# A fused two-layer decoder kernel: the norm's split by 256-column parts, high parts first, and the output by parts

## The chip, the cores and the metric

The kernel runs as one program on one core of one Trainium2 chip. The metric is the device time of one execution in microseconds (us); the figure for the kernel before is the median of three runs. The core's engines are PE (TensorE, matrix multiplication), DVE (VectorE), ACT (ScalarE), POOL (GpSimd) and SP (SyncE, which here only issues DMAs).

## The reference

Two layers over 256 rows of 1024 columns, in float32. `moba`, `nsa` and `gla` stand for three kinds of attention; their insides don't matter here.

```python
def rms_norm(x, gain):
    xf = x.astype(jnp.float32)
    y = xf * lax.rsqrt(jnp.mean(xf * xf, axis=-1, keepdims=True) + NORM_EPS)
    return (y * gain.astype(jnp.float32)).astype(x.dtype)
```

Each layer computes `h = rms_norm(x)`, one wide projection of h for all branches, the three branches, `z = sum_i sigmoid(gate_i(h)) * (branch_i @ P_i)` and `x = x + z @ W_out`; then `x = x + ConvFFN(rms_norm(x))`, where the FFN projects up to 2 x 2816 columns, convolves and gates them, and projects down by `w_down`. The result is x after the second layer.

## The kernel before

x lives in SBUF as `xs`, 128 partitions x 2 row tiles t x 1024 columns. Each float32 product runs on PE as three matmuls on rounded operands: high by high, high by low and low by high. For weights, SP loads a block `raw` of 1024 elements per partition, ACT casts it to `whi`, and DVE or POOL or both subtract to get `wlo`; a rule in the planner (`low`, L303) cuts the columns between the two. For activations, `hh` is the high and `hl` the low part of the turned, gain-scaled x.

A phase is a list of chunks (a 512- or 256-column piece of a weight matrix); `run_phase` (L407) walks over blocks of k-tiles, three matmuls per k-tile and piece, and after each k step calls `tick()`, which advances the generators in the lists `urgent` and `normal`. Everything that isn't a main matmul is such a generator: the work of a chunk's end (`done_...`), the splits, the attention. Its `yield from avail(...)` or `ready(...)` waits until a planner's clock (class `Plan`, L51, with a cost per instruction) says that the data will be there; so the planner's costs decide after which matmul the generator's instructions are put. The order of each engine's instructions is thus fixed when the program is built, and hardware semaphores do the waiting. All instructions are recorded through one helper, so every one has line L163 in the profile; tiles tell them apart.

The order of chunks in the up projection is `split_order(3, 4)`: the first four k-tiles of three chunks, then their last four. So k-tiles 0 to 3 are needed first, and all of the first half's work comes from columns 0 to 511 of x. The input projection of layer 1 uses `split_order(2, 4)`; the output projection `split_order(2, 4)`, the down projection chunk after chunk.

The change touches the seam between two projections. `done_out` (L1426) is the end of a chunk of the output projection (w_out) or the down projection (w_down): for half c (512 columns) it adds the two PSUM banks `pd` (one for each t) to `xs`, then runs `nxt(c)`, which is `after_mixer` (L1437) or `after_ffn` (L1442). Both run `norm_half` (L641): for each of two parts j of 256 columns, i.e. two k-tiles, it takes a bank `pst` (semaphore `sem_ps`, three banks), lets PE turn the part (`x_T`, L624, four transposes), and splits k-tile by k-tile: `norm_hi` (ACT, hh), `norm_lo` (DVE, hl), and again. Then `norm_sq` (L658) squares the half's columns on ACT, and after the second half `norm_rs` (L665) makes the root (POOL) and turns it (PE). After the last layer, `after_ffn` issues the output DMAs instead, one for each t.

Four places are meant below. A: 229 to 250 us, from layer 0's output projection to its up projection. B: 426 to 470, from its down projection to layer 1's input projection. C: 643 to 664, as A in layer 1. D: the end.

Of the kernel before, what the change touches and what calls it, by code (L numbers as in the profile page):

```python
# [13 lines left out]
OP = mybir.AluOpType  # L14
# [166 lines left out]
def trunk_kernel(ctx, tc, x, rel_bias, attn_norm, w_in, moba_q_norm, moba_k_norm,  # L181
# [19 lines left out]
    sem_pd, sem_po, sem_ps, sem_t = Sem(4), Sem(1), Sem(3), Sem(NT)  # L201

    def take(s, n=1):
        while True:
            t = s.at(n)
            if t is not None and t <= plan.t["PE"]:
                break
            plan.step = max(plan.step, t or 0.0)
            yield
        s.take(n)  # L210

    def give(s, n=1):
        s.free += [plan.step] * n
# [4 lines left out]
    def pst():  # L218
        return ps.tile([128, 512], F32, name="pst", tag="pst")

    def tt():
        return tp.tile([128, 512], F32, name="tt", tag="tt", bufs=NT)

    plan = Plan()
    V, A, G, PE, SP = (Eng(plan, e, g) for e, g in (("V", nc.vector), ("A", nc.scalar), ("G", nc.gpsimd),
                                                    ("PE", nc.tensor), ("S", nc.sync)))

    def avail(*aps):
        while max(plan.get(a) for a in aps) > plan.t["PE"]:
            plan.step = max([plan.step] + [plan.get(a) for a in aps])  # L230
            yield
# [7 lines left out]
    def bc(ap, shape):  # L239
        return ap.to_broadcast(shape)  # L240
# [98 lines left out]
    urgent, normal = [], []  # L339
    flags = set()  # L340
# [53 lines left out]
    def wait(*fl):  # L394
        for f in fl:
            while f not in flags:
                yield
# [88 lines left out]
    xs = cst.tile([128, 2, D], F32, name="xs")  # L486
# [127 lines left out]
    def norm_state(key):  # L614
        st = {}
        st["h"] = hp.tile([128, 8, S], F32R, name="hh", tag="hh")
        st["l"] = hp.tile([128, 8, S], F32R, name="hl", tag="hl")
        st["ss"] = at.tile([128, 2, 2], F32, name="ss", tag="ss", bufs=2)
        st["rs"] = at.tile([128, 2], F32, name="rs", tag="rs", bufs=2)
        st["rsh"] = at.tile([128, 2], F32, name="rsh", tag="rsh", bufs=2)  # L620
        st["rsB"] = at.tile([128, 1, S], F32, name="rsB", tag="rsB", bufs=2)
        st["key"] = key
        return st

    def x_T(c):

        p = pst()
        for k in range(2):
            for t in range(2):
                PE.transpose(p[:, k * 256 + t * 128:k * 256 + t * 128 + 128],  # L630
                             xs[:, t, c * 256 + k * 128:c * 256 + k * 128 + 128], ident)
        return p

    def norm_hi(st, c, k, p, g):
        A.activation(st["h"][:, 2 * c + k], p[:, k * 256:k * 256 + 256], AF.Copy, scale=g[:, 2 * c + k:2 * c + k + 1])

    def norm_lo(st, c, k, p, g):
        V.scalar_tensor_tensor(st["l"][:, 2 * c + k], p[:, k * 256:k * 256 + 256], g[:, 2 * c + k:2 * c + k + 1],
                               st["h"][:, 2 * c + k].bitcast(F32), op0=OP.mult, op1=OP.subtract)

    def norm_half(st, c, l, goff):  # L641

        yield from wait(("par", l))
        g = par[l][0][:, goff:goff + 8]
        for j in (2 * c, 2 * c + 1):
            yield from take(sem_ps)
            p = x_T(j)
            yield
            for k in range(2):
                norm_hi(st, j, k, p, g)  # L650
                norm_lo(st, j, k, p, g)
            give(sem_ps)
            flags.add((st["key"], j))
        yield from norm_sq(st, c)
        if c:
            yield from norm_rs(st)

    def norm_sq(st, c):  # L658
        yield from take(sem_t)
        q = tt()  # L660
        for t in range(2):
            A.activation(q, xs[:, t, c * 512:c * 512 + 512], AF.Square, accum_out=st["ss"][:, t, c:c + 1])
        give(sem_t)

    def norm_rs(st):  # L665
        ms = at.tile([128, 2], F32, name="ms", tag="ms", bufs=2)
        V.tensor_tensor(ms, st["ss"][:, :, 0], st["ss"][:, :, 1], op=OP.add)
        V.tensor_scalar(ms, ms, 1.0 / D, EPS, op0=OP.mult, op1=OP.add)
        G.tensor_tensor(st["rs"], ms, mhalf[:, :2], op=OP.pow)
        yield  # L670
        yield from avail(st["rs"])
        V.tensor_scalar(st["rsh"], st["rs"], 0.5, None, op0=OP.mult)
        flags.add((st["key"], "rs"))
        yield from take(sem_ps)
        p = pst()
        for t in range(2):
            PE.transpose(p[:, t * 128:t * 128 + 128], bc(st["rs"][:, t:t + 1], [128, 128]), ident)
        yield
        A.copy(st["rsB"][:, 0], p[:, :256])
        give(sem_ps)  # L680
        flags.add((st["key"], "rsB"))
# [10 lines left out]
    def make_layer(l):  # L692
        key = lambda *a: (l,) + a
        st = {}
# [728 lines left out]
                give(sem_t, 2)  # L1423
            return f

        def done_out(c, nxt):  # L1426
            def f(p):
                for t in range(2):
                    xv = xs[:, t, c * 512:c * 512 + 512]
                    V.tensor_tensor(xv, p[t], xv, op=OP.add)  # L1430
                give(sem_pd, 2)
                yield
                yield from avail(*(xs[:, t, c * 512:c * 512 + 512] for t in range(2)))
                yield from nxt(c)
            return f

        def after_mixer(c):  # L1437
            if "n2" not in st:
                st["n2"] = norm_state(key("n2"))
            yield from norm_half(st["n2"], c, l, 8)  # L1440

        def after_ffn(c):  # L1442
            if l + 1 < L:
                nx = layers[l + 1]
                if "n1" not in nx["st"]:
                    nx["st"]["n1"] = norm_state((l + 1, "n1"))
                yield from norm_half(nx["st"]["n1"], c, l + 1, 0)
            else:
                o2 = out.rearrange("b (t p) d -> p (b t) d", p=128)
                for t in range(2):  # L1450
                    SP.dma_start(o2[:, t, c * 512:c * 512 + 512], xs[:, t, c * 512:c * 512 + 512])
                yield


# [71 lines left out]
        for c in range(2):  # L1526
            for br, (w, nk, kx, fl_) in enumerate(((w_branch_moba, 2, 0, "moba"), (w_branch_nsa, 2, 2, "nsa"),
# [3 lines left out]
                                   lambda k, fl_=fl_: key(fl_)))  # L1531
        ph_out = [Chunk("A", 512, 8, wload(w_out[l], [(c * 512, 512)]), lambda: (st["zh"], st["zl"], 0),
                        done_out(c, after_mixer), lambda k: key(("z", k // 2))) for c in range(2)]
        ph_up = []
        for j in range(11):
# [119 lines left out]
    for l, ly in enumerate(layers):  # L1655
        st = ly["st"]
# [12 lines left out]
    k = 0  # L1669
# [51 lines left out]
```

## Time and profile before

| | |
|---|---|
| median of 3 runs | 843.26 us (842.91 to 844.48) |
| profiled execution | 844.73 us |
| its span in the profile | 842.9 us |
| mean granted TensorE clock | 0.996 |
| PE busy | 831.8 us (99%) |
| DVE busy | 571.0 us (68%) |
| ACT busy | 430.1 us (51%) |
| POOL busy | 418.0 us (50%) |

Times inside the profile count from the span's start. An idle time in brackets behind a row is that of the engine just before the instruction, with the instruction that ended it. Matmuls overlap in the record: one of 512 columns is shown with 0.39 us, but the next starts 0.23 later. The granted clock is the share of TensorE's full 2.4 GHz; 0.50 is 1.2 GHz.

### The profile page before, as it was taken

The numbers are of one execution on the slowest core, as the hardware profiler recorded it, in microseconds if no ns is written. First come the engines' busy times: TensorE is split into PE (matmuls) and PEld (weight loads), VectorE is DVE, ScalarE is ACT, GpSimd is POOL, SyncE is SP. The second block draws the span as 40 slices with busy tenths as digits, with TensorE's granted clock in tenths as the row PEclk, the third lists the DMA queues.
The fourth block names the chain that finished last, engine by engine and source line by source line (L and its number), as shares of the span: only waits on it lengthen the run. The fifth ranks groups of instructions, "written<-read, shape, count | busy, mean of one in ns | idle before, by whom it ended". The sixth has DMA issues, their size and how long they took to land.

```text
span 842.9 us, 13919 instructions
## 1 busy us (share of the span) xinstructions
PE 831.8 (99%) x5173; PEld 741.0 (88%) x5173; DVE 571.0 (68%) x880; ACT 430.1 (51%) x667; POOL 418.0 (50%) x338
## 2 busy tenths in 40 slices
PE   8999999999999999999999999999999999999998
PEld 7789888888899999988897898888887999999886
DVE  4676887458657888774457478766585688777642
ACT  5565546554456544544456444655544664545431
POOL 2435653456535655565425265435564265665652
PEclk9999999999999999999999999999999999999999
DMA  6893534545545656655568435434556556665560
GB/s 212 234 317 108 152 114 131 150 165 185 180 147 180 197 176 175 201 179 199 156 178 245 128 100 150 130 121 150 181 174 196 153 165 188 196 184 190 191 210 26
DMA packets 109976, 143.57 MB, mean 170 GB/s; under 512 B 13677, under 2 KB 71380, under 8 KB 109780
## 3 DMA queue, kind: packets, MB, share of 16 engines
q1 hardware_dynamic: 109892, 142.68, 54.7%
q8 instruction: 41, 0.67, 0.3%
q14 instruction: 27, 0.22, 0.1%
q10 hardware_dynamic: 16, 0.00, 0.0%
HBM read 141.60 MB, written 2.63 MB: 171 GB/s over the span
## 4 chain that ended last, share of the span: by engine, by line
PE 91%; DVE 3%; issue 2%; POOL 2%; ACT 1%; DMA 0%; SPq 0%; POOLq 0%; DVEq 0%; ACTq 0%
PE pd L163 80%; PE pst L163 9%; PE po L163 2%; POOL wlo L163 2%; DVE wlo L163 1%; ACT whi L163 1%; DVE tt L163 1%; DVE xs L163 0%; POOL tt L163 0%; DVE hl L163 0%; ACT hh L163 0%; DVE boot L163 0%; DVE m L163 0%; DMA tt<-in_moba_k_norm_dram 0%; DVE kn L163 0%
## 5 line engine op out<-in xcount | busy, mean ns | idle before, releaser
L163 ACT CAST whi<-raw 128x1024 fp32r<-128x1024 f32 (+3 forms) x268 | 271.4, 1017 | 285.1 <-PE pd L163 178.0
L163 POOL TENSOR_TENSOR wlo<-raw,whi 128x192 fp32r<-128x192 f32 (+7 forms) x221 | 264.3, 1199 | 302.9 <-ACT whi L163 264.5
L163 DVE TENSOR_TENSOR wlo<-raw,whi 128x832 fp32r<-128x832 f32 (+8 forms) x266 | 286.3, 1087 | 136.6 <-ACT whi L163 136.0
L163 PE MATMUL pd<-hh,whi 128*128 128x256 f32 x768 | 218.8, 285 | 0.3
L163 PE MATMUL pd<-hl,whi 128*128 128x256 f32 x768 | 217.5, 283 | 1.4 <-DVE hl L163 1.4
L163 PE MATMUL pd<-hh,wlo 128*128 128x256 f32 x768 | 217.3, 283 | 0.0
L163 PE MATMUL pd<-whi,hh 128*128 128x512 f32 (+3 forms) x512 | 204.4, 399 | 1.4 <-DVE grp L163 0.5
L163 PE MATMUL pd<-wlo,hh 128*128 128x512 f32 (+3 forms) x512 | 194.4, 380 | 1.0 <-POOL wlo L163 0.5
L163 PE MATMUL pd<-whi,hl 128*128 128x512 f32 (+3 forms) x512 | 193.3, 378 | 0.0
L163 PEld LDWEIGHTS pd<-hh,whi 128*128 128x128 f32 x768 | 147.4, 192 | 1.9 <-issue 0.7
L163 PEld LDWEIGHTS pd<-hl,whi 128*128 128x128 f32 x768 | 147.3, 192 | 1.9 <-DVE hl L163 1.8
L163 PEld LDWEIGHTS pd<-hh,wlo 128*128 128x128 f32 x768 | 147.3, 192 | 0.0
L163 PEld LDWEIGHTS pd<-whi,hh 128*128 128x128 f32 x512 | 97.9, 191 | 20.0 <-issue 3.7
L163 PEld LDWEIGHTS pd<-whi,hl 128*128 128x128 f32 x512 | 97.7, 191 | 17.5
L163 PEld LDWEIGHTS pd<-wlo,hh 128*128 128x128 f32 x512 | 98.1, 192 | 16.3 <-DVE wlo L163 1.5
L163 DVE SCALAR_TENSOR_TENSOR tt<-tt,pt 128x255 f32<-128x255 f32 x88 | 69.6, 811 | 1.6
L163 PE MATMUL pd<-whi,fh 128*128 128x512 f32 x176 | 68.7, 390 | 0.0
L163 PE MATMUL pd<-wlo,fh 128*128 128x512 f32 x176 | 68.5, 389 | 0.0
L163 PE MATMUL pd<-whi,fl 128*128 128x512 f32 x176 | 68.5, 389 | 0.0
L163 POOL TENSOR_TENSOR fl<-tt,fh 128x512 fp32r<-128x512 f32 x22 | 45.7, 2079 | 30.7 <-DVE fh L163 28.1
L163 ACT ACTIVATE tt<-tt,nm 128x128 f32<-128x128 f32 (+1 forms) x48 | 21.3, 445 | 45.8 <-DVE nm L163 45.8
L163 PEld LDWEIGHTS pd<-whi,fl 128*128 128x128 f32 x176 | 33.0, 188 | 6.9
(208 smaller groups left out, 803.9 us busy)
## 6 DMA issues: line engine op xcount, KB each, us to landing
raw<-in_w_up_dram SPq DMA_DIRECT2D x88, 512.0 KB
raw<-in_w_in_dram SPq DMA_DIRECT2D x84, 512.0 KB
raw<-in_w_down_dram SPq DMA_DIRECT2D x44, 512.0 KB
raw<-in_w_out_dram SPq DMA_DIRECT2D x16, 512.0 KB
raw<-in_w_branch_gla_dram SPq DMA_DIRECT2D x8, 512.0 KB
raw<-in_w_in_dram SPq DMA_DIRECT2D x8, 396.0 KB
raw<-in_w_branch_moba_dram SPq DMA_DIRECT2D x4, 512.0 KB
raw<-in_w_branch_nsa_dram SPq DMA_DIRECT2D x4, 512.0 KB
```

Source lines behind the costliest of these rows:

```text
L163: return g(*args, **kw)
```

## The change

`norm_half` becomes `norm_part`, which does one part of 256 columns: both high parts (ACT), then both low parts (DVE). `done_out` adds to x by 256 columns, in the order columns 0 to 255 of t=0, of t=1, columns 256 to 511 of t=0, of t=1, and after each pair appends to `urgent` a generator of its own, `turn`, that waits for the part's x and then runs `norm_part`, or the output. The squares come after the odd parts. The output goes by parts, both t in one DMA; it is four DMAs of 256 KB before and after. The argument `scale` of the new `done_out` stays unused.

```diff
@@ -638,22 +638,23 @@
         V.scalar_tensor_tensor(st["l"][:, 2 * c + k], p[:, k * 256:k * 256 + 256], g[:, 2 * c + k:2 * c + k + 1],
                                st["h"][:, 2 * c + k].bitcast(F32), op0=OP.mult, op1=OP.subtract)
 
-    def norm_half(st, c, l, goff):
+    def norm_part(st, j, l, goff):
 
         yield from wait(("par", l))
         g = par[l][0][:, goff:goff + 8]
-        for j in (2 * c, 2 * c + 1):
-            yield from take(sem_ps)
-            p = x_T(j)
-            yield
-            for k in range(2):
-                norm_hi(st, j, k, p, g)
-                norm_lo(st, j, k, p, g)
-            give(sem_ps)
-            flags.add((st["key"], j))
-        yield from norm_sq(st, c)
-        if c:
-            yield from norm_rs(st)
+        yield from take(sem_ps)
+        p = x_T(j)
+        yield
+        for k in range(2):
+            norm_hi(st, j, k, p, g)
+        for k in range(2):
+            norm_lo(st, j, k, p, g)
+        give(sem_ps)
+        flags.add((st["key"], j))
+        if j % 2:
+            yield from norm_sq(st, j // 2)
+            if j == 3:
+                yield from norm_rs(st)
 
     def norm_sq(st, c):
         yield from take(sem_t)
@@ -1423,32 +1424,40 @@
                 give(sem_t, 2)
             return f
 
-        def done_out(c, nxt):
+        def done_out(c, nxt, scale=None):
             def f(p):
-                for t in range(2):
-                    xv = xs[:, t, c * 512:c * 512 + 512]
-                    V.tensor_tensor(xv, p[t], xv, op=OP.add)
-                give(sem_pd, 2)
+                for q in (0, 1):
+                    for t in range(2):
+                        xv = xs[:, t, c * 512 + q * 256:c * 512 + q * 256 + 256]
+                        pv = p[t][:, q * 256:q * 256 + 256]
+                        if scale is None:
+                            V.tensor_tensor(xv, pv, xv, op=OP.add)
+                        else:
+                            V.scalar_tensor_tensor(xv, pv, scale(t), xv, op0=OP.mult, op1=OP.add)
+                    if q:
+                        give(sem_pd, 2)
+                    urgent.append(turn(2 * c + q, nxt))
                 yield
-                yield from avail(*(xs[:, t, c * 512:c * 512 + 512] for t in range(2)))
-                yield from nxt(c)
             return f
 
-        def after_mixer(c):
+        def turn(j, nxt):
+            yield from avail(*(xs[:, t, j * 256:j * 256 + 256] for t in range(2)))
+            yield from nxt(j)
+
+        def after_mixer(j):
             if "n2" not in st:
                 st["n2"] = norm_state(key("n2"))
-            yield from norm_half(st["n2"], c, l, 8)
-
-        def after_ffn(c):
+            yield from norm_part(st["n2"], j, l, 8)
+
+        def after_ffn(j):
             if l + 1 < L:
                 nx = layers[l + 1]
                 if "n1" not in nx["st"]:
                     nx["st"]["n1"] = norm_state((l + 1, "n1"))
-                yield from norm_half(nx["st"]["n1"], c, l + 1, 0)
+                yield from norm_part(nx["st"]["n1"], j, l + 1, 0)
             else:
                 o2 = out.rearrange("b (t p) d -> p (b t) d", p=128)
-                for t in range(2):
-                    SP.dma_start(o2[:, t, c * 512:c * 512 + 512], xs[:, t, c * 512:c * 512 + 512])
+                SP.dma_start(o2[:, :, j * 256:j * 256 + 256], xs[:, :, j * 256:j * 256 + 256])
                 yield
 
 
```

The split sets the instruction order anew. On ACT at C, with the semaphores that each instruction waits for (`hh` is the second norm's high part, `ss` its sums of squares, `pst_...` one bank each), the kernel before has:

```order
L163 ACTIVATE hh_6488<-pst_6494,pt_2827 128x256 [waits PE_49]
L163 ACTIVATE hh_6488<-pst_6494,pt_2827 128x256 [waits DVE_49]
L163 CAST whi_6531<-raw_6469 128x1024 [waits DMAHW3_49,PE_49,Pool_49]
L163 ACTIVATE hh_6488<-pst_6516,pt_2827 128x256
L163 ACTIVATE hh_6488<-pst_6516,pt_2827 128x256 [waits DVE_49]
L163 ACTIVATE tt_6553,ss_6490<-xs_86 128x512
L163 ACTIVATE tt_6553,ss_6490<-xs_86 128x512 [waits Activation_49]
L163 CAST whi_6575<-raw_6499 128x1024 [waits DMAHW4_49,PE_49,Pool_49]
```

and the changed kernel at the same place:

```order
L163 ACTIVATE hh_6495<-pst_6501,pt_2831 128x256 x2
L163 ACTIVATE hh_6495<-pst_6509,pt_2831 128x256 [waits PE_49]
L163 ACTIVATE hh_6495<-pst_6509,pt_2831 128x256
L163 ACTIVATE tt_6535,ss_6497<-xs_86 128x512 [waits DVE_49]
L163 ACTIVATE tt_6535,ss_6497<-xs_86 128x512 [waits DVE_49,Activation_49]
L163 CAST whi_6550<-raw_6479 128x1024 [waits DMAHW3_49,PE_49,Pool_49]
L163 CAST whi_6587<-raw_6514 128x1024 [waits DMAHW4_49,PE_49,Pool_49]
```

The cast that stood between the two pairs of hh now follows the squares, and no hh waits for DVE any more.

On DVE at C, from the last adds of w_out's first half to the norm's last low parts (- before, + changed):

```order
-L163 TENSOR_TENSOR xs<-pd,xs 128x512 x2
-L163 TENSOR_TENSOR wlo<-raw,whi 128x832 x2
+L163 TENSOR_TENSOR xs<-pd,xs 128x256 x4
+L163 TENSOR_TENSOR wlo<-raw,whi 128x832
 L163 SCALAR_TENSOR_TENSOR hl<-pst,pt,hh 128x256 x2
-L163 TENSOR_TENSOR xs<-pd,xs 128x512 x2
+L163 TENSOR_TENSOR wlo<-raw,whi 128x576
+L163 SCALAR_TENSOR_TENSOR hl<-pst,pt,hh 128x256 x2
+L163 TENSOR_TENSOR xs<-pd,xs 128x256 x4
+L163 TENSOR_TENSOR wlo<-raw,whi 128x768
 L163 TENSOR_TENSOR wlo<-raw,whi 128x832
 L163 SCALAR_TENSOR_TENSOR hl<-pst,pt,hh 128x256 x4
```

The low parts of the first half stand ahead of the second half's adds, with a shorter wlo between them, and the adds are four instead of two.

On DVE in layer 1's input projection (B, 460 to 466 us; `kn` is normalised k, `nqs` the scale of q, `grp` a group of gated columns, the first `tt` an operand of the compressed keys and values, the second scaled q):

```order
-L163 TENSOR_TENSOR kn<-a_4609,kss 128x2x64 x4
+L163 TENSOR_TENSOR kn<-a_4618,kss 128x2x64 x4
 L163 TENSOR_TENSOR wlo<-raw,whi 128x832
 L163 TENSOR_TENSOR tt<-pst,pt 64x256 x4
+L163 TENSOR_TENSOR tt<-pd,nqs 128x256 x2
 L163 SCALAR_TENSOR_TENSOR grp<-pd,rsB 128x512
-L163 TENSOR_TENSOR wlo<-raw,whi 128x320
-L163 TENSOR_TENSOR tt<-pd,nqs 128x256 x2
+L163 TENSOR_TENSOR wlo<-raw,whi 128x640
```

The two `tt` that free their `pd` banks by way of `nqs` moved ahead of `grp`, and the `wlo` behind it grew.

In layer 1's input projection the changed program has the transposes of `rs` 9 main matmuls earlier, and those of the gate's operands 6 to 12 earlier; the transposes of `kn` stand at the same count of main matmuls. At A and C the transposes of x's parts 0 and 1 stand 3 and 6 main matmuls earlier, those of part 2 stand 6 later, those of part 3 stay.

## Rows read from the trace of the kernel before

**Rows 1.** The head of the profile's page: the span, and busy time, share of the span and number of instructions by engine.

```profile
span 842.9 us, 13919 instructions
...
PE   831.8 (99%) x5173; PEld 741.0 (88%) x5173; DVE 571.0 (68%) x880; ACT 430.1 (51%) x667; POOL 418.0 (50%) x338
```

**Rows 2.** PE's waits, grouped by what ended them: us in total, times, longest us.

```profile
PE pd L163 <- DVE hl L163: 1.4, 2, 0.7
...
PE pd L163 <- DVE grp L163: 0.5, 1, 0.5
PE pst L163 <- DVE tt L163: 0.5, 1, 0.5
```

**Rows 3.** The timeline at C, all engines: start, us, engine, operation, out<-in, count, and the idle time before with its releaser.

```profile
649.14 0.48 ACT L163 ACTIVATE hh<-pst,pt 128x256 fp32r<-128x256 f32 x1 [1.11 <-DVE hl L163]
...
649.65 0.48 DVE L163 SCALAR_TENSOR_TENSOR hl<-pst,pt,hh 128x256 fp32r<-128x256 f32 x1 [0.55 <-ACT hh L163]
...
650.02 0.28 PE L163 MATMUL pd<-hh,whi 128*128 128x256 f32 x1
...
650.06 1.28 DVE L163 TENSOR_TENSOR xs<-pd,xs 128x512 f32<-128x512 f32 x2
...
650.26 1.05 ACT L163 CAST whi<-raw 128x1024 fp32r<-128x1024 f32 x1 [0.64 <-PE pd L163]
...
651.22 0.47 ACT L163 ACTIVATE hh<-pst,pt 128x256 fp32r<-128x256 f32 x1
651.33 0.28 PE L163 MATMUL pd<-hh,wlo 128*128 128x256 f32 x1
651.35 1.02 DVE L163 TENSOR_TENSOR wlo<-raw,whi 128x832 fp32r<-128x832 f32 x1
...
652.80 0.47 ACT L163 ACTIVATE hh<-pst,pt 128x256 fp32r<-128x256 f32 x1 [1.12 <-DVE hl L163]
...
653.51 0.60 PE L163 MATMUL pst<-ident,xs 128*128 128x128 f32 x4
...
653.86 0.37 PE L163 MATMUL pd<-hh,whi 128*128 128x256 f32 x1
```

**Rows 4.** The timeline of PE at A.

```profile
237.65 0.28 PE L163 MATMUL pd<-hh,wlo 128*128 128x256 f32 x1
...
239.85 0.60 PE L163 MATMUL pst<-ident,xs 128*128 128x128 f32 x4
```

**Rows 5.** Prices: two hh in a row on ACT's timeline after A, and from the view of tile xs its adds (duration in ns, least, median and most, and the first and last start in us).

```profile
243.10 0.84 ACT L163 ACTIVATE hh<-pst,pt 128x256 fp32r<-128x256 f32 x2 [0.55 <-DVE hl L163]
...
L163 DVE TENSOR_TENSOR xs<-pd,xs x16: 680/684/692, 229.5 to 839.2; 128x512 f32<-128x512 f32 x16
```

**Rows 6.** The timeline at B of DVE, with the root on POOL.

```profile
435.88 0.49 DVE L163 SCALAR_TENSOR_TENSOR hl<-pst,pt,hh 128x256 fp32r<-128x256 f32 x1 [0.55 <-ACT hh L163]
...
437.69 0.70 POOL L163 TENSOR_TENSOR rs<-ms,mhalf 128x2 f32<-128x2 f32 x1 [8.48 <-DVE ms L163]
...
460.56 1.29 DVE L163 TENSOR_TENSOR kn<-a,kss 128x128 f32<-128x128 f32 x4
...
462.71 1.74 DVE L163 TENSOR_TENSOR tt<-pst,pt 64x256 f32<-64x256 f32 x4
...
464.48 0.69 DVE L163 SCALAR_TENSOR_TENSOR grp<-pd,rsB 128x512 f32<-128x512 f32 x1
...
465.48 0.75 DVE L163 TENSOR_TENSOR tt<-pd,nqs 128x256 f32<-128x256 f32 x2
```

**Rows 7.** The timeline at B of PE.

```profile
461.90 0.55 PE L163 MATMUL pst<-ident,kn 128*128 128x128 f32 x3 [0.42 <-DVE kn L163]
...
463.61 1.08 PE L163 MATMUL pst<-tt,w 128*128 128x30 f32 x8 [0.46 <-DVE tt L163]
...
465.22 0.80 PE L163 MATMUL pd<-whi,hh 128*128 128x512 f32 x1 [0.53 <-DVE grp L163]
...
466.67 1.05 PE L163 MATMUL pst<-ident,tt 128*128 128x128 f32 x4
...
468.59 0.39 PE L163 MATMUL pd<-whi,hh 128*128 128x512 f32 x1
...
468.82 0.39 PE L163 MATMUL pd<-wlo,hh 128*128 128x512 f32 x1
```

**Rows 8.** Busy time by stretch at B: length, busy us of PE, PEld, DVE, ACT and POOL (with instructions begun), granted clock, share of the DMA engines, GB/s.

```profile
464.00:465.00 1.00, 0.69 (x7) 0.57 (x6) 0.95 (x3) 0.00 (x0) 0.32 (x1) 0.95 0.84 191
465.00:468.00 3.00, 2.78 (x9) 2.29 (x10) 2.01 (x6) 0.24 (x1) 0.00 (x0) 0.50 0.71 208
468.00:469.00 1.00, 1.00 (x5) 0.84 (x4) 0.00 (x0) 0.45 (x1) 0.00 (x0) 0.85 0.59 227
```

**Rows 9.** The same view at the stalls of A and C.

```profile
238.00:239.00 1.00, 0.39 (x1) 0.19 (x1) 1.00 (x2) 0.00 (x1) 1.00 (x1) 1.00 0.48 167
...
652.00:653.00 1.00, 0.30 (x2) 0.18 (x2) 0.77 (x2) 0.20 (x1) 0.82 (x1) 1.00 0.09 31
```

**Rows 10.** The timeline of the end; the last row's us run from the first issue to the end of the second, an issue taking 0.36.

```profile
838.53 1.37 DVE L163 TENSOR_TENSOR xs<-pd,xs 128x512 f32<-128x512 f32 x2 [8.04 <-PE pd L163]
...
838.78 0.39 PE L163 MATMUL pd<-whi,fl 128*128 128x512 f32 x1
839.25 1.04 SPq L163 DMA_DIRECT2D out_dram<-xs  x2
```

## The prediction

> **What bounds the kernel now.** I read the page's head first, then PE's waits by releaser, then the stretches in which those waits fall. PE is busy for 831.8 of 842.9 us [rows 1], so only work that makes PE wait, or that stands behind its last matmul, can move the time. PE's waits by releaser are few. The largest is for hl, the low part of a norm: 1.4 us in two waits [rows 2]. The waits for grp, tt and kn, 0.4 to 0.5 each, fall in one place (464 us). The profiled execution took 844.73 us, 1.47 above the median of 843.26; its span of 842.9 leaves 1.83 around it. All terms are differences, so I take their sum from the median.
>
> The diff acts at four places: A (236 to 240 us) and C (650 to 654), where w_out of layer 0 and 1 ends and the up projection starts; B (426 to 470), where layer 0's FFN ends and layer 1's input projection starts; D, the end.
>
> **A and C: the split of the norm.** In C the rows show two engines that hand over by turns. ACT writes hh (high) of k-tile 0, DVE writes hl (low) from the same PSUM tile, and only then does ACT write hh of k-tile 1: it idles 1.11 us until DVE's hl. DVE then idles 0.55 until that hh [rows 3]. One pair costs three handovers. On top, a cast stands between the pairs on ACT and the next chunk's adds to x (650.06, 1.28 us for two) on DVE. So hh of the second pair starts at 651.22 and its second one at 652.80. PE reads one k-tile in 6 matmuls. Twelve had started by 651.33, 11 steps after 650.02, hence 0.119 apart; 18 stand ahead of the next transposes, which were due at 651.33 + 7 x 0.119 = 652.16 and came at 653.51. **C loses 1.35 us.** In A the twelfth matmul starts at 237.65, the transposes were due at 238.48 and came at 239.85 [rows 4]: **1.37 lost.**
>
> After the change ACT has four hh in a row, waiting for PE's transposes alone, because the transposes of both pairs stand 3 and 6 matmuls earlier (a matmul of 512 columns issues every 0.23 us, the last two of [rows 7], so 0.7 and 1.4 us). The cast and the squares go behind them. DVE has wlo, two hl, a shorter wlo, two hl, and only then the next adds. Two hh in a row took 0.84 us [rows 5], 0.42 each; one hl takes 0.48. Walked through C: the adds of the first chunk take four instructions, 0.4 us more than two, so the cast ahead ends near 648.0 rather than 647.6; hh at 647.9, 648.35, 648.75, 649.2; hl of the first pair end near 649.7 and 650.1, those of the second, behind a wlo of 576 columns (an estimate of 0.65 to 0.75, from 1.02 for 832 columns [rows 3]), near 651.2 and 651.6. PE wants the low parts one matmul after each k-tile's start: 650.14, 650.85, 651.57 and 652.28. The margins are 0.4 to 0.7 us, the smallest at the first k-tile's low part and the third's; the first k-tile pays for the new order, as its low part waits for both high parts (0.42). The moved transposes of the third part come 6 matmuls later, and their x is ready by 652.8. The moved cast is for a block three ahead, 8 us later. Nothing else is late next, so A and C give **-2.7**; if a margin is missed by 0.4, 0.4 of each comes back (-1.9).
>
> **B: two steps off.** The pairs there are split while w_down still runs, and PE does not wait for them. Today's last hl ends at 436.4 and the root on POOL starts at 437.69 [rows 6]. With four hh and four hl in a row and the cast behind them, it starts some 3 us earlier; the planner puts the transposes of rs 9 matmuls earlier, and the gate chain of the linear attention (tanh, exponent, scan) moves with it. What follows on DVE is one chain: kn at 460.56, a wlo, four tt to 464.45, grp at 464.48, tt from pd and nqs at 465.48 [rows 6]. I followed each wait of the new order with the old durations: one wlo now lies ahead of the scan's copies, the rest is the same, and kn starts near 459.85, 0.7 earlier. PE's transposes of kn then lose their wait of 0.42. The next matmuls, w, start today at 463.61 after 0.46 [rows 7]; PE could start them at 462.73, DVE lets them at 462.9: 0.7 gained. The pd bank for which PE waited until 465.22 is freed by grp today; the new order has tt from pd and nqs before grp, the bank PE needs is that one, and it is free at 464.15: 1.07 gained. I take **-1.0**; bounds -1.2 and 0, the latter if POOL's nqs or ACT comes last. On SP the load of the gate's weights and the small loads of w go out a place or two earlier among the weight blocks; all are issued well before w is first read at 463.61, so nothing waits for them.
>
> **The clock in B.** The granted clock is 1.00 until PE's third wait, then 0.95, 0.50 for 465 to 468 and 0.85 [rows 8]: three us at 1.2 GHz rather than 2.4. From 465.22 to 468.59 PE issued six matmuls of 512 columns and four transposes [rows 7]; at full clock these take 6 x 0.23 plus 0.35 (C's four, 653.51 to 653.86 [rows 3]), 1.73, so the fall costs 3.37 - 1.73 = 1.64. Before it PE had waited 0.42, 0.46 and 0.53 within four us. In A and C PE waits 1.35 in one go and the clock stays at 1.00 [rows 9]. With one of B's three waits gone and the other two cut to some 0.2, what is left (0.4) is far below what A and C bear. So I take the fall as gone: **-1.6**, bounds -1.6 and 0.
>
> The Trainium skill speaks against this: TensorE: Matmul & The Clock Gate, section "A second HAM failure mode: psum-queue depth-cycling", tells of a kernel in which short idle moments between groups of matmuls were enough for the clock to swing. By that rule the remaining waits may still throw the clock, and the sum would lack the 1.6; A and C do not bear it out, B's three waits in a row do.
>
> **D: the end.** The last matmul starts at 838.78 and takes 0.39. DVE's two adds end at 839.9, and the second output DMA is issued at 839.25 + 1.04 - 0.36 = 839.93 [rows 10]. After the change the first add runs beside the last matmul, as now, but the second waits for that matmul (839.17) and two more follow it before the last DMA can go: 3 x 0.40 to 840.4. An add of 512 columns takes 0.684 [rows 5]; half of it, 0.34, gives +0.3, a 256-column instruction like hl, 0.48, gives +0.7. I take **+0.5**. Rows of 1 KB instead of 2 KB are not in the trace; that the last DMA now flies alone may return 0.3. The output of the first half lies at 809 us beside w_down and costs nothing.
>
> The Trainium skill's page DMA: Bandwidth & Descriptors, section "Anatomy of one DMA — SWDGE (gpsimd) path", fits a DMA as about 2.0 us plus its bytes at 436 GB/s, for another path: an estimate of 2.6 for 256 KB. The trace has 842.9 - 839.93 = 2.97 for today's last one. By the page D would be +0.1 rather than +0.5.
>
> Eight more adds per layer cost DVE some 0.3 us for each of the chunks; PE does not wait for DVE there, and DVE is busy 68% [rows 1].
>
> Sum: -2.7 - 1.0 - 1.6 + 0.5 = -4.8; 843.26 - 4.8 = **838.5 us**.
>
> **Rivals.** (1) *The clock still falls in B.* For it: waits remain there, and the same transposes and narrow matmuls lie around them. Against it: rows 9. Then 838.5 + 1.6 = **840.1**. (2) *The change does not do what it says in A and C*: the new adds (four, 0.4 us longer) push the cast and with it every hh, so the margins of 0.4 to 0.7 are not there, half the stall stays, and B's chain, bound by another engine, gives nothing: -1.35 + 0.5 gives 842.4, with spread **841 to 843.3**. For it: the margins are small against a walk of single steps. (3) *Slower: the first pair's low part becomes the new stall.* It now stands behind both high parts, and these behind the longer adds and a cast. PE starts the up projection at 650.02 whatever they do. If the first low part ends later than 651.5, 1.35 after PE wants it, PE waits there for longer than today, and the later k-tiles with it; two times 1.3 on top of today's 1.35, nothing from B and 0.5 at D: 843.26 + 2.6 + 0.5 = **846.4**. Against it: hl of the first pair would have to come 1.8 us later than my walk; today it ends at 650.1, behind three handovers.
>
> **How the numbers follow.** The forecast has 0.52, rival 1 0.25, rival 2 0.14, rival 3 0.09. A measurement of this kernel tells 0.2% (1.7 us) from no change, so faster is below 841.6, slower above 844.9. Forecast and rival 1 are faster (0.77), rival 2 to a quarter (0.03) and else the same (0.11), rival 3 slower. The range reaches from 837.4 (the forecast with B at -1.2, D at +0.1 and a little from shorter waits near 464 us) through rival 1 to 842.2, most of rival 2; what is left out is rival 3 and the tails.
>
> **What would show it.** In A and C: four hh without idle time on ACT, transposes of the third part on time, no hl among PE's waits. If hl stays there, the row's k-tile tells rival 2 (third k-tile) from rival 3 (first). In B: kn some 0.7 us earlier against the start of w's phase, the wait for grp gone, and the granted clock at 1.00 through 470 us; a stretch at 0.50 is rival 1. In D: the last output DMA issued some 1.3 us after the last matmul's end, against 0.8 now. The forecast is wrong if PE waits for an engine in a place that the diff does not touch, since the planner re-plans all that follows.

## The result and the profile after

The changed kernel takes 838.74 us (median of 6 executions, 836.88 to 839.63) against 843.0 us (6 executions, 841.71 to 844.48) of the kernel before; the ratio is 0.9948 with a 95% interval of 0.9934 to 0.9961, 3.3 to 5.6 us. Its profiled execution took 839.14 us with a span of 837.4. One execution of the kernel before, beside the later runs, took 1643.88 us and is left out of everything below.

The head of the page, which answers to [rows 1], and PE's waits by releaser, which answer to [rows 2]:

```profile
span 837.4 us, 13965 instructions
...
PE   827.2 (99%) x5173; PEld 737.6 (88%) x5173; DVE 570.9 (68%) x896; ACT 428.8 (51%) x667; POOL 416.0 (50%) x338
```
```profile
PE pd L163 <- DVE wlo L163: 0.8, 4, 0.3
...
PE pst L163 <- DVE tt L163: 0.4, 1, 0.4
PE pd L163 <- DVE tt L163: 0.4, 1, 0.4
```

The waits for hl, kn and grp are gone; a new one for the second tt (scaled q) has come, and the one for the first tt is 0.4 instead of 0.5. The waits for wlo all lie in the first 23 us; two that the first profile of the kernel before doesn't have are in its second profile too (6.23 and 8.99 us), so the change did not bring them.

C, all engines, after (answers to [rows 3]):

```profile
643.16 1.56 ACT L163 ACTIVATE hh<-pst,pt 128x256 fp32r<-128x256 f32 x4
...
644.03 0.88 DVE L163 SCALAR_TENSOR_TENSOR hl<-pst,pt,hh 128x256 fp32r<-128x256 f32 x2 [2.89 <-ACT hh L163]
644.82 0.75 DVE L163 TENSOR_TENSOR wlo<-raw,whi 128x576 fp32r<-128x576 f32 x1
645.48 0.87 DVE L163 SCALAR_TENSOR_TENSOR hl<-pst,pt,hh 128x256 fp32r<-128x256 f32 x2
646.27 1.41 DVE L163 TENSOR_TENSOR xs<-pd,xs 128x256 f32<-128x256 f32 x4
...
645.16 0.28 PE L163 MATMUL pd<-hh,whi 128*128 128x256 f32 x1
...
648.03 0.60 PE L163 MATMUL pst<-ident,xs 128*128 128x128 f32 x4
```

The four hh run through, the last hl ends at 646.35, and only then do the adds come. PE's first matmul of the up projection starts at 645.16; 24 matmuls later, at 648.03, come the transposes of the third part: (648.03 - 645.16) / 24 = 0.12, the pace of 0.119 that PE had before it waited. Nothing waits.

B, PE and DVE, after (answers to [rows 6, 7]):

```profile
458.66 0.60 PE L163 MATMUL pst<-ident,kn 128*128 128x128 f32 x4
...
460.37 1.08 PE L163 MATMUL pst<-tt,w 128*128 128x30 f32 x8 [0.42 <-DVE tt L163]
461.81 0.47 PE L163 MATMUL pd<-whi,hh 128*128 128x512 f32 x1 [0.35 <-DVE tt L163]
462.11 0.40 PE L163 MATMUL pd<-wlo,hh 128*128 128x512 f32 x1
```
```profile
457.31 1.30 DVE L163 TENSOR_TENSOR kn<-a,kss 128x128 f32<-128x128 f32 x4
...
459.47 1.74 DVE L163 TENSOR_TENSOR tt<-pst,pt 64x256 f32<-64x256 f32 x4
461.24 0.76 DVE L163 TENSOR_TENSOR tt<-pd,nqs 128x256 f32<-128x256 f32 x2
461.91 0.68 DVE L163 SCALAR_TENSOR_TENSOR grp<-pd,rsB 128x512 f32<-128x512 f32 x1
```

The next matmul after 461.81 follows 0.30 later, and the clock holds, as the stretches show (answers to [rows 8]; columns as there):

```profile
460.00:461.00 1.00, 0.63 (x6) 0.63 (x6) 0.95 (x3) 0.00 (x0) 0.90 (x1) 1.00 0.76 187
461.00:462.00 1.00, 0.65 (x6) 0.56 (x6) 0.97 (x4) 0.00 (x0) 0.00 (x0) 1.00 0.83 245
...
465.00:468.00 3.00, 3.00 (x23) 2.18 (x22) 1.28 (x4) 0.70 (x1) 1.43 (x1) 1.00 0.43 160
```

The end (answers to [rows 10]):

```profile
832.34 0.42 DVE L163 TENSOR_TENSOR xs<-pd,xs 128x256 f32<-128x256 f32 x1 [8.04 <-PE pd L163]
...
832.60 0.39 PE L163 MATMUL pd<-whi,fl 128*128 128x512 f32 x1
833.02 1.09 DVE L163 TENSOR_TENSOR xs<-pd,xs 128x256 f32<-128x256 f32 x3 [0.25 <-PE pd L163]
833.47 1.04 SPq L163 DMA_DIRECT2D out_dram<-xs  x2
```

The page gives the span to 0.1 us; a view of the stretch that runs to the end gives it to 0.01, here for the kernel before and the changed one:

```profile
838.00:842.94 4.94, 1.17 (x6) 0.63 (x4) 1.37 (x2) 0.00 (x0) 0.00 (x0) 1.00 0.28 106
```
```profile
832.00:837.36 5.36, 0.98 (x5) 0.48 (x3) 1.51 (x4) 0.00 (x0) 0.00 (x0) 1.00 0.29 98
```

From the last matmul's end (832.99) to the last DMA's issue (833.47 + 1.04 - 0.36 = 834.15) it is 1.16 us, 0.76 before; from there to the span's end 3.21, 3.01 before. The end is 0.60 us longer, 0.40 in the issue and 0.20 in the landing. (The expectations below have 0.68 and 0.28 for these 0.60 and 0.20, from spans rounded to 0.1 us.)

**A ledger.** All kernels here issue the same 4368 main matmuls (those that write pd) in the same order. So the start of matmul n can be compared between two profiles, and the difference, stretch by stretch, tells where time went. Each number is the stretch's length less that in the first profile of the kernel before, in us. The stretches: to matmul 107 (35 us), to 840 (before A), A to 960, to 2340, B's waits to 2379, what follows them to 2390, to 3024, C to 3144, then from the last matmul's start to the span's end. Where a stretch is left out, no profile differs by more than 0.03.

| profile | start | 107 to 840 | A | B: waits | B: after | 2390 to 3024 | C | end | span |
|---|---|---|---|---|---|---|---|---|---|
| before, second | -1.35 | 0.05 | -0.02 | -0.02 | -1.23 | -0.02 | 0.03 | 0.01 | 840.4 |
| before, third | -0.72 | 0.05 | 0.00 | -0.02 | -1.21 | 0.85 | 0.02 | 0.00 | 841.9 |
| changed | -1.07 | 0.00 | -1.36 | -0.96 | -1.46 | 0.01 | -1.33 | 0.61 | 837.4 |
| changed, second | -0.69 | 0.07 | -1.36 | -0.97 | -1.47 | 0.01 | -1.33 | 0.59 | 837.8 |
| e1_order_only | -0.19 | 0.06 | -0.01 | -0.02 | -1.21 | 0.89 | 0.01 | 0.01 | 842.5 |
| e2_parts_only | -1.50 | 0.92 | -0.99 | -0.88 | -1.47 | 0.85 | -0.94 | 0.60 | 839.5 |
| e3_old_end | -1.49 | 0.93 | -1.35 | -0.98 | -1.46 | 0.89 | -1.33 | 0.00 | 838.1 |
| e4_old_B | -0.65 | 0.07 | -1.36 | -0.01 | 0.19 | -0.02 | -1.33 | 0.61 | 840.5 |
| e6_out_rows | -0.67 | 0.05 | -1.36 | -0.97 | -1.47 | 0.01 | -1.33 | 0.74 | 837.9 |
| e7_streams | -0.39 | 0.02 | -1.38 | -1.03 | -1.46 | 0.01 | -1.34 | 0.01 | 837.3 |
| e8_dve_alone | -0.37 | 0.92 | -1.35 | -0.98 | -1.46 | 0.01 | -1.32 | 0.59 | 839.0 |
| e9_end_no_tie | -0.56 | 0.04 | -1.35 | -0.97 | -1.46 | 0.02 | -1.33 | 0.00 | 837.3 |

A, C, the waits of B and the end repeat to 0.1 us wherever the instructions are the same; the start, the two stretches of 0.9 and "B: after" vary between executions of one kernel. What the start does is read from its matmuls of 272 columns: in the four profiles with -1.07 or less, one of them of the kernel before, they issue every 0.12 us from 6.5 us on, in the others every 0.23 until 9 to 11 us. Both come in profiles of one kernel, so this is no effect of the change.

### The profile page after: what moved, and what is told of

It is laid out like the page before. It is cut to its first block, busy times and chain, and to the rows that moved or that the text cites. A ratio compares the mean times of both kernels' runs of the same rounds, so it can differ in the third digit from the quotient of the medians.

```text
span 837.4 us, 13965 instructions
## 1 busy us (share of the span) xinstructions
PE 827.2 (99%) x5173; PEld 737.6 (88%) x5173; DVE 570.9 (68%) x896; ACT 428.8 (51%) x667; POOL 416.0 (50%) x338
## 4 chain that ended last, share of the span: by engine, by line
PE 96%; DMA 2%; DVE 1%; ACT 1%; issue 0%; SPq 0%; POOL 0%; DVEq 0%; ACTq 0%
PE pd L163 85%; PE pst L163 9%; PE po L163 2%; DMA xs<-in_x_dram 1%; DMA raw<-in_w_in_dram 0%; DVE wlo L163 0%; ACT whi L163 0%; DMA rb<-in_rel_bias_dram 0%; SPq L163 0%; DVE tt L163 0%; DVE kn L163 0%; ACT hh L163 0%; DVE boot L163 0%; POOL wlo L163 0%; DVE xs L163 0%
## 5 line engine op out<-in xcount | busy, mean ns | idle before, releaser
L163 POOL TENSOR_TENSOR wlo<-raw,whi 128x192 fp32r<-128x192 f32 (+6 forms) x221 | 261.9, 1189 | 307.0 <-ACT whi L163 268.9
```

What stands on the lines that cost most here:

```text
L163: return g(*args, **kw)
```

## The experiments

Two theories of A and C stood against each other after the result. **Queue:** PE waited because ACT's cast and DVE's adds and wlo stood between the first pair's parts and the second's; a stream for each part moves them behind. **Handover:** PE waited because ACT and DVE took turns within a pair.

**The order alone, the streams alone.** e1_order_only is the kernel before with this:

```diff
             for k in range(2):
                 norm_hi(st, j, k, p, g)
+            for k in range(2):
                 norm_lo(st, j, k, p, g)
```

> The kernel before with one thing changed: in each pair both high parts, then both low parts; adds, streams and output stay by 512 columns. Theory (queue): at A and C PE waits because ACT's cast and DVE's adds and wlo stand between the first pair's parts and the second's; here they still do, so A and C each keep 1.0 to 1.35 us of their stall, and B, whose order of instructions stays that of before but for single places, keeps its waits and its stretch at clock 0.50: 842.4 to 843.2, against 843.0 before and 838.7 changed. Rival (handover): the stall is the three handovers within a pair; without them A and C lose nearly all of it, 2.7 us together: 840.2 to 840.6, with B as before.

Measured: 843.73 us (12 executions), ratio 1.0009 (0.9998 to 1.0019); A and C gain nothing, -0.01 and 0.01. Its C, ACT, DVE and PE:

```profile
649.78 1.05 ACT L163 CAST whi<-raw 128x1024 fp32r<-128x1024 f32 x1 [1.87 <-issue]
650.74 0.83 ACT L163 ACTIVATE hh<-pst,pt 128x256 fp32r<-128x256 f32 x2
...
651.81 0.87 DVE L163 SCALAR_TENSOR_TENSOR hl<-pst,pt,hh 128x256 fp32r<-128x256 f32 x2
...
652.34 0.38 PE L163 MATMUL pd<-hl,whi 128*128 128x256 f32 x1 [0.70 <-DVE hl L163]
653.04 0.60 PE L163 MATMUL pst<-ident,xs 128*128 128x128 f32 x4
```

Both hh of the second pair now follow each other, and PE waits just as long: the pair starts behind the cast, and its hl behind the wlo. The handover rival falls. The streams also move the transposes of both parts 3 and 6 matmuls forward. That alone couldn't help the second pair: in the kernel before its transposes, the row below, were done 2.4 us before its first hh at 651.22 [rows 3].

```profile
648.19 0.60 PE L163 MATMUL pst<-ident,xs 128*128 128x128 f32 x4
```

e2_parts_only is the changed kernel with the old turns:

```diff
         for k in range(2):
             norm_hi(st, j, k, p, g)
-        for k in range(2):
             norm_lo(st, j, k, p, g)
```

> The changed kernel with the old order within a pair (high, low, high, low). Every engine has the changed kernel's order but for those turns, so each second high part waits for DVE again. Queue theory: A and C lose 0.2 to 0.5 us each, at the fourth k-tile's low part; B and D as in the changed kernel, clock at 1.00 near 462 us: 839.1 to 839.8. Handover rival: A and C lose 1.35 each again, 841.4.

Measured: 840.8 us (12), ratio 0.9973 (0.9962 to 0.9984). A and C gain 0.99 and 0.94, as the queue theory had it, but not for the reason given: no hl makes PE wait. ACT and DVE of e2 at C, and a row of PE's waits:

```profile
645.94 0.84 ACT L163 ACTIVATE hh<-pst,pt 128x256 fp32r<-128x256 f32 x2 [0.55 <-DVE hl L163]
...
648.54 0.48 DVE L163 SCALAR_TENSOR_TENSOR hl<-pst,pt,hh 128x256 fp32r<-128x256 f32 x1 [0.54 <-ACT hh L163]
```
```profile
PE pst L163 <- POOL rs L163: 0.4, 2, 0.2
```
```profile
658.20 0.43 PE L163 MATMUL pst<-ident,rs 128*128 128x128 f32 x2 [0.18 <-POOL rs L163]
```

The last hl ends at 649.02, before PE wants it (the fourth k-tile starts 18 x 0.12 = 2.16 after 646.92, at 649.08). What the turns cost comes later, in PE's waits for the root rs, the second of which is shown: 0.38 us at each place by the ledger, all of it at one matmul, the 948th and the 3132nd. There, 6 matmuls earlier than in the kernel before, the planner has put the transposes of rs in the changed kernel and in e2 alike. So the parts' streams are worth 1.0 and the order 0.4 on top of them, and without the streams the order is worth nothing. Whether the 0.4 would go too with the transposes of rs in their old place (6 x 0.12 = 0.72 us later, an estimate) was not run.

**Adds by 512, streams kept.** e7_streams, which also keeps the old end of the last layer:

```diff
-                for q in (0, 1):
-                    for t in range(2):
-                        xv = xs[:, t, c * 512 + q * 256:c * 512 + q * 256 + 256]
...
+                for t in range(2):
+                    xv = xs[:, t, c * 512:c * 512 + 512]
+                    V.tensor_tensor(xv, p[t], xv, op=OP.add)
+                give(sem_pd, 2)
+                for q in (0, 1):
                     urgent.append(turn(2 * c + q, nxt))
```

> The changed kernel with x updated by 512 columns as before (two adds for a chunk), the two parts still turned by a stream of their own, high parts first, and the end as before. Theory: the streams put the transposes of both parts earlier and the cast, the adds and the wlo behind them, so A and C still gain 1.2 to 1.4 us each and the adds by 256 columns give nothing; with the end at 4.1 us, within 0.5 us of e3_old_end. Rival: the adds by 256 columns are what gets x early enough; A and C keep 0.5 us or more of their stall.

Measured: 839.19 us (6), ratio 0.9951 (0.9937 to 0.9965); A -1.38, C -1.34, B as changed, end as before. The adds by 256 columns give nothing at A, B and C; all of it is the streams and the order.

**The end.** e3_old_end keeps the old end of the last layer:

```diff
-                       done_out(c, after_ffn), lambda k: key(("f", k // 2))) for c in range(2)]
+                       (done_out(c, after_ffn) if l + 1 < L else done_half(c, after_half)), lambda k: key(("f", k // 2))) for c in range(2)]
```

with `done_half` and `after_half` as in the kernel before.

> The changed kernel, but the last layer's end as before: adds of 512 columns, one output DMA for each t with rows of 2 KB. Theory: the end from the last matmul's start to the span's end goes from 4.8 us back to 4.1, 0.7 shorter, all else alike: 838.0, the fastest of all. Rival: the end's length is a matter of when the last bytes land and not of the last issue, 838.7 as the changed kernel.

The end is back at the 4.16 us of the kernel before. The median, 839.67 us (6), ratio 0.9959 (0.9943 to 0.9975), does not show it: in the profiled execution two waits of 0.9 stand against it, of which below.

e6_out_rows:

```diff
-                    urgent.append(turn(2 * c + q, nxt))
+                    if nxt is not None:
+                        urgent.append(turn(2 * c + q, nxt))
+                if nxt is None:
+                    o2 = out.rearrange("b (t p) d -> p (b t) d", p=128)
+                    for t in range(2):
+                        SP.dma_start(o2[:, t, c * 512:c * 512 + 512], xs[:, t, c * 512:c * 512 + 512])
```

In the last layer `nxt` is None, so both output DMAs are issued after the four adds.

> The changed kernel with its four adds by 256 columns at the end, but the output DMAs by t with rows of 2 KB as before, both issued after all four adds. Theory: of the 0.68 us at the end, 0.40 is the later last issue and 0.28 the DMA of 1 KB rows; with 2 KB rows the time from the last matmul's start to the end is 4.5 us instead of 4.8. Rival: the landing after the last issue is the same for both row lengths, and as the first DMA is issued later too, 4.8 or more.

Measured: 839.69 us (5), ratio 0.9959 (0.9946 to 0.9972). Its end, and that of the changed kernel's second profile:

```profile
833.02 0.39 PE L163 MATMUL pd<-whi,fl 128*128 128x512 f32 x1
833.45 1.09 DVE L163 TENSOR_TENSOR xs<-pd,xs 128x256 f32<-128x256 f32 x3 [0.26 <-PE pd L163]
834.23 0.83 SPq L163 DMA_DIRECT2D out_dram<-xs  x2
```
```profile
833.03 0.39 PE L163 MATMUL pd<-whi,fl 128*128 128x512 f32 x1
...
833.91 1.05 SPq L163 DMA_DIRECT2D out_dram<-xs  x2
```

With rows of 2 KB the last issue lies at 834.23 + 0.83 - 0.36 = 834.70 and the span ends 3.2 later (837.9); with 1 KB rows at 834.60, and also 3.2 later (837.8). The theory that the short rows make the landing longer isn't borne out. It isn't ruled out either: in e6 the two DMAs are issued 0.47 us apart instead of 0.69. What makes the landing 3.2 instead of 3.0 stays open.

**The clock at B.** e4_old_B gives layer 0's down projection its old end, the rest is the changed kernel:

```diff
-                       done_out(c, after_ffn), lambda k: key(("f", k // 2))) for c in range(2)]
+                       (done_half(c, after_half) if l + 1 < L else done_out(c, after_ffn)), lambda k: key(("f", k // 2))) for c in range(2)]
```

> The changed kernel, but layer 0's down projection ends as before (adds by 512 columns, one stream, high and low by turns); A, C and D as changed. Theory: layer 1's input projection gets the order of before back, with PE's waits of 0.4 to 0.5 us for kn, tt and grp, and after them the clock at 0.50 for some 3 us: 1.0 + 1.5 = 2.5 slower than the changed kernel, 841.2, with the granted clock 0.5 in that place. Rival: the clock's fall has another cause than these waits (it does not come back), 839.7.

Measured: 842.23 us (12), ratio 0.9985 (0.9974 to 0.9997). PE's three waits at B return to within 0.01, and with them the fall; PE of e4, and its stretches:

```profile
459.97 0.55 PE L163 MATMUL pst<-ident,kn 128*128 128x128 f32 x3 [0.41 <-DVE kn L163]
461.68 1.08 PE L163 MATMUL pst<-tt,w 128*128 128x30 f32 x8 [0.46 <-DVE tt L163]
463.29 0.50 PE L163 MATMUL pd<-whi,hh 128*128 128x512 f32 x1 [0.53 <-DVE grp L163]
```
```profile
464.00:465.00 1.00, 1.00 (x7) 0.83 (x5) 1.00 (x3) 0.00 (x0) 0.00 (x0) 0.51 0.40 52
465.00:468.00 3.00, 3.00 (x10) 2.40 (x9) 0.08 (x1) 0.91 (x2) 0.00 (x0) 0.59 0.50 161
```

Against the changed kernel it loses 0.95 in the waits and 1.65 behind them (ledger). So far the theory holds. But e1 has the same waits and its clock did not fall. So the kernel before was profiled twice more:

> The kernel before, profiled once more. Theory: PE's waits for hl at A and C (1.36 and 1.34 us lost) and for kn, tt and grp at B (0.42, 0.46, 0.53) come again to 0.05 us, since they follow from the order; the fall of the clock after B's waits comes only in some executions. Rival: the fall is as fixed as the waits, and 465 to 468 us show 0.50 again.

> The kernel before, profiled a third time, to the same end: the waits at A, B and C as in the first two, the clock at B either at 1.00 or fallen, and the wlo of 320 columns near 118 and 532 us at 0.49 or 1.35.

They took 842.27 and 843.7 us. The waits at A, B and C are those of [rows 2, 7] to 0.02, and the clock at B holds in both; the second profile has

```profile
463.90 0.51 PE L163 MATMUL pd<-whi,hh 128*128 128x512 f32 x1 [0.53 <-DVE grp L163]
```
```profile
465.00:468.00 3.00, 3.00 (x18) 2.62 (x19) 0.69 (x2) 1.71 (x2) 0.00 (x0) 1.00 0.56 175
```
```profile
466.04 0.40 PE L163 MATMUL pd<-whi,hh 128*128 128x512 f32 x1
```

The rival (the fall is as fixed as the waits) falls. The mean granted clock of each execution tells about how often it comes: 0.996 and 0.995 in the two profiles with the fall, 0.997 and 0.998 in those without. Of the 50 executions of the kernel before that ran beside e1 to e9 11 have 0.996 or less (median 844.37 us; the other 39, 842.98), of e1's 12 two, of e4's 12 ten; of the 53 executions of the changed kernel, e2, e3 and e6 to e9, whose waits there are cut, none. The 11 may be too few: every profile has one more stretch at 0.50 near 30 us, in the start, and an execution without that one (means of 0.999 and 1.000 point to some) would hide a fall at B behind 0.998. Where the waits are cut no fall was seen, and where they stand they don't decide it; what does is not shown.

**The changed kernel again.**

> The changed kernel once more, beside further runs of before. Theory: the terms that every run has are -1.36 at A, -1.34 at C, -1.04 for PE's waits at B and +0.68 at the end, 3.1 us in all; the 1.5 of the clock come on top only against those runs of before in which the clock falls at B (mean granted clock 0.996, 7 of 29), so the ratio of the medians lies at 0.996 to 0.9965. Rival: the clock's term belongs to every run, 4.6 us, ratio 0.9945.

Measured: 839.11 us (6), ratio 0.9948 (0.9934 to 0.9962), the rival's number. But its reason can't be right, as the clocks above show. The theory's 0.996 to 0.9965 lies at and beyond the interval's upper end; with 0.60 for the end, the 0.24 of the new order behind B's waits and the fall's share of 0.3 it would have been some 0.9957, inside.

**A tie between DVE and POOL.** Three of the first six profiles lose 0.9 us in a place that no kernel here changes, near 529 us, and two of them near 118. DVE and POOL of e3_old_end, then of the changed kernel:

```profile
528.08 1.35 DVE L163 TENSOR_TENSOR wlo<-raw,whi 128x320 fp32r<-128x320 f32 x1
...
528.07 1.01 POOL L163 TENSOR_TENSOR wlo<-raw,whi 128x384 fp32r<-128x384 f32 x1 [0.30 <-DVE qz L163]
```
```profile
527.54 0.49 DVE L163 TENSOR_TENSOR wlo<-raw,whi 128x320 fp32r<-128x320 f32 x1
...
527.54 1.37 POOL L163 TENSOR_TENSOR wlo<-raw,whi 128x384 fp32r<-128x384 f32 x1 [0.31 <-DVE qz L163]
```

```profile
529.57 0.47 PE L163 MATMUL pd<-wlo,hh 128*128 128x512 f32 x1 [0.72 <-DVE wlo L163]
```

Both instructions become free when DVE ends qz. Where POOL is 0.01 us ahead, DVE's takes 1.35 us instead of 0.49, and PE waits for a wlo behind it (the last row, of e3). The 13 profiles have the pair 23 times: 7 times POOL is 0.01 ahead and DVE's takes 1.35, 16 times the two begin together or DVE is ahead, and it takes 0.49. e8_dve_alone takes the POOL instruction away, in layer 1:

```diff
             m = best[1]
+            self.seen = getattr(self, "seen", 0) + (m == 704)
+            if self.seen == 2 and m == 384:
+                m, self.seen = 0, 3
             if m < c:
```

> The changed kernel with one low part of weights (384 columns on POOL, 640 on DVE, near 529 us) on DVE alone. Theory: in some runs POOL's 384 columns start some 10 ns before a wlo of 320 columns on DVE, which then takes 1.35 us instead of 0.49 and makes PE wait 0.9 us; without the POOL instruction DVE takes 0.49 in every run, the wait is gone, and the median is 0.3 to 0.6 us below the changed kernel's on the same chip. Rival: the wait comes from something else on DVE (an operand that is late), and it stays.

Measured: 839.82 us (6), ratio 0.9955 (0.9939 to 0.997). Near 528 us DVE takes 0.49 and nothing is lost (0.01), but the same tie in layer 0, near 118 us, went the other way in this execution (0.92), and the median is not lower than the changed kernel's. e9_end_no_tie is e3_old_end with the same done in both layers:

```diff
             m = best[1]
+            self.seen = getattr(self, "seen", False) or m == 704
+            if self.seen and m == 384:
+                m, self.seen = 0, False
             if m < c:
```

> The changed kernel with the end as in e3_old_end, and in both layers the low part of weights that has 384 columns on POOL (near 118 and 528 us) on DVE alone. Theory: the end gives 0.68, and DVE's wlo of 320 columns takes 0.49 us in both layers in every run, so that neither wait of 0.9 us can come: 0.7 to 1.6 below the changed kernel, 837.2 to 838.4, the fastest of all. Rival: with the whole 1024 columns on DVE, DVE is late for the next chunk there (0.4 us or more at PE), and only the end's 0.7 is left, 838.1 to 838.6.

Measured: 839.11 us (6, 837.41 to 839.35), ratio 0.9943 (0.9925 to 0.9961). DVE takes 0.49 in both layers, neither stretch loses more than 0.04, and the end is 4.15: without the start its profile is 5.08 us below the first of before, the changed one's 4.51. The median is above what either theory gave; that it is faster than the changed kernel is shown stretch by stretch in the profile, not by the times.

## Why the prediction came true, and where not

The time (838.5 forecast, 838.74 measured) and the direction are right; the sum got there with one term that doesn't belong to every execution, and that the two times lie 0.24 apart is in part luck.

**A and C, -2.7:** measured -1.36 and -1.33. Right in size, and so was that the cast, the squares and the adds go behind the parts. Wrong is the weight on the three handovers: taken away alone (e1) they give nothing. The part that the order of a pair does give, 0.4 at each place beside the streams, lies at the transposes of rs (e2), which the prediction didn't name at A and C. The margins were larger than the walk's 0.4 to 0.7: hh started 2.0 us ahead of the up projection's first matmul (643.16 and 645.16), as walked (2.1), but the four low parts ended near 644.51, 644.91, 645.96 and 646.35, and PE wanted them at 645.28, 645.99, 646.70 and 647.42: 0.7 to 1.1.

**B's waits, -1.0:** measured -0.96, with the chain that was followed, but not in the shares forecast. Between the two profiles 0.73 are gained at the transposes of kn, which no longer wait, and only 0.22 behind them: the two waits that are left, put at some 0.2 each, are 0.42 and 0.35. Another 0.2 comes at the four transposes of q's tt, in "B: after".

**The clock, -1.6:** here the prediction failed in a step. "All terms are differences, so I take their sum from the median" took the fall, most likely, out of an execution that hadn't had it. The profiled execution of before, 1.47 above the median, was one in which the clock fell, and it has the slowest start of all profiles. Of the execution in the middle (843.26) no clock is on record, but of the 50 later ones 39 show no fall in their mean clock, with a median of 842.98.

The size was off as well. The fall costs 1.2 us (ledger, before against its second and third profile; the other 0.24 of "B: after" comes with the new order), not 1.64: at 1.00 the same matmuls take 466.04 - 463.90 = 2.14 us in the second profile, not the 1.73 of the walk. With 11 of 50 executions that is 0.3 us on average, not 1.6. Taken from the profiled execution's own 844.73, the sum would have given 839.9; without the clock, from the median, 840.1.

That the fall goes when the waits are cut was right: no fall was seen with the waits cut. The argument from A and C, which bear a longer wait, doesn't explain it, as B bears its own waits in most executions too. Rival 1 had the clock fall again; it didn't. The rule of the Trainium skill that stood beside it (TensorE: Matmul & The Clock Gate, section "A second HAM failure mode: psum-queue depth-cycling"), that short idle moments can be enough, agrees with the executions of before that fell; at the two waits that the changed kernel keeps, 0.42 and 0.35 us, no execution bears it out.

**The end, +0.5:** measured +0.60, of which 0.40 is the later issue (forecast 0.5) and 0.20 the landing, where the prediction had hoped for a gain of up to 0.3 because the last DMA flies alone. It doesn't: it is issued 0.68 us after its neighbour (1.04 - 0.36), as in [rows 10]. The Trainium skill's fit for a DMA (DMA: Bandwidth & Descriptors, section "Anatomy of one DMA — SWDGE (gpsimd) path"), an estimate of 2.6 us for another path, is further from the 3.2 of the trace than the 3.0 of the kernel before (2.97 in the prediction, from the rounded span) was.

**The range.** Its lower end, 837.4, does not follow from the terms named: 838.5 less 0.2 at B and 0.4 at D is 837.9, and no row gives the other 0.5.

**What stays open.** The terms that every execution has make -1.36 - 1.33 - 0.96 - 0.24 + 0.60 = -3.3, with the fall's share -3.6. The medians differ by 4.3 and, in the second comparison, 4.5. So the forecast of -4.8 counted 1.2 us too many, and the medians have 0.7 to 0.9 that no row explains. The two ratios' intervals reach down to 3.2 us, so there is no contradiction, and other medians miss the ledger the other way (e3's ratio makes 3.5 us where its terms, with the fall's share, make 4.2). Whether the ties and the start, which cost up to 0.9 each and 1.5, come out better for the changed kernel more often, the runs don't settle.

## What to carry to other kernels

Here the wait between engines was set by what stood in their queues ahead of the work, and not by how two of them took turns within it: give each piece that a consumer needs separately its own place in the order, and try the order inside a piece by itself before crediting it. Before a stall or a fall of the clock in a profile is put into a sum, see whether it is there in other executions of the same kernel, and subtract it from the execution that had it. Where the program order is fixed, comparing the start of the same matmul in two profiles tells 0.1 us apart where medians don't tell 1.

## What the hardware showed that was not expected

With the same instructions and the same waits (0.41, 0.46, 0.53 us) the granted clock fell to 1.2 GHz in some executions of one program and held 2.4 in others: by the mean clocks in some 11 of 50 for the kernel before and in 10 of 12 for e4, where A's gain brings the place 1.36 us closer to the start. A and C, where PE loses 1.35 us in one go, never show it in the four profiles with these waits.

Two elementwise instructions on DVE and POOL that become free at the same moment are decided by some 10 ns, and the one behind pays: DVE's 320 columns took 0.49 us when the two began together and 1.35 when POOL was 0.01 ahead, while POOL's 384 took 1.36 or 1.01. PE lost 0.9 us to it.
